# A decoder layer on one core: attention steps in the order scores, filling, values, transposes, filling; the third branch's first inputs in another ring; a variance as float32r

## The chip, the cores and the metric

The kernel runs on one core of a Trainium2 chip. The metric is the device time of one execution in microseconds (us); the lower the better. Each comparison uses several runs, and one further execution is recorded by the hardware profiler. The engines are called as the profile calls them: PE (matrix multiplications), PEld (PE's weight loads), DVE (vector), ACT (scalar), POOL (GpSimd) and SP (the queue that issues most transfers).

## The reference

One layer, 1024 tokens of 1024 channels, float32. It is a feed-forward half step, then a mixer with three branches, then a second feed-forward half step.

```python
u = rms_norm(h, mix_pre_g)
p_rwkv, p_swa, q_mem, gate_logits = _split(u @ w_in, IN_SIZES)
y_a = rwkv7_mix(p_rwkv, ...)                 # recurrence, 8 heads of 64
y_b = sliding_window_gqa_sinks(...)          # window of 128 tokens, 8 heads of 64
y_c = memory_cross_attention(q_mem, ...)     # 256 memory tokens, 4 heads of 128
g_a, g_b, g_c = _split(jax.nn.sigmoid(gate_logits + gate_b), (D, D, D))
merged = g_a * (y_a @ w_branch[0]) + g_b * (y_b @ w_branch[1]) + g_c * (y_c @ w_branch[2])
h = h + rms_norm(merged @ w_out, mix_post_g)
```

`rwkv7_mix` ends with a normalization of each head: the variance over its 64 channels, then a scaling with its reciprocal root.

## The kernel before, in words

Channels lie on the 128 partitions and tokens on the free axis, in halves `h` = 0 and 1 of 512 tokens. A product in full precision is three matrix multiplications in float32r (`mm3`, L348 to L350): weights and inputs are kept as a rounded part `hi` and a rest `lo`, and `hi*hi + hi*lo + lo*hi` is summed in PSUM. ACT makes the `hi` (L277 for weights, L454 for inputs), DVE the `lo` (L279 and L455). A multiplication of plain float32 goes through PE in two passes, and the trace counts both.

The mixer's small, latency-bound pieces (recurrence, normalization, attention) are interleaved by hand with large products. A generator, `filling` (L1252), yields the matmuls of the gates, of the first branch (RWKV, index 0) and of the second (memory, index 2, by `BRANCHES = (0, 2, 1)`). `fill(n, behind)` draws some `n` of them behind a given instruction, in whole steps of its generator. In this part of the program PE's order is the order of the code.

**PSUM.** There are two rings of four banks, `mm` for the large products and `bg` for the rest. Every score bank (`sc`, `msc`), transposed bank (`ptr`, `mptr`) and output bank (`pv`, `mpv`) takes the next of the four `bg` banks and waits until the tile that had it before has been read.

**Attention.** `attention` (L1428) takes 16 blocks of 128 tokens: 8 of memory attention, then 8 of the window. For block `i`, before the change, it calls `values` of block i-1, `turn` of block i, `scores` of block i+1, half of the filling, `load` of block i+2, and the other half. `scores` issues the score matmuls (L93) and the whole softmax: for the window four banks copied by ACT (L126) and DVE (L127), a maximum (L131), the exponentials on ACT, the sum and reciprocal (L138, L139) and eight scalings on DVE (L141). `turn` transposes the probabilities on PE (L96) into two `ptr` banks; ACT copies each (L151), and for window blocks from the second on DVE multiplies each by a mask (L154). `values` multiplies with the values (`pv`) and `y_out` (L1447) copies the result out and sends it to memory `y_d`. `load` brings the queries `qs`, and in a window block the rotation (`rotate`, L1404 to L1406) runs on DVE. One window iteration has 54 matmuls of filling; DVE also works for the filling's weights (L279), for sums of the second feed-forward's weights (`ws`, L611 to L614) and for the first branch's merging (L1492).

**Variance.** `rwkv_finish` (L1190) squares each of 8 halves of the recurrence's output on ACT (L1206, tile `ysq`, three buffers), sums them within each head by a float32 matmul with a matrix of ones (L1213), and takes the logarithm on ACT (L1215), which needs another table of functions first. Filling stands behind each pair: 6, 6 and 12 matmuls, then 30.

**Branches.** `branch_strip` (L1473) loads a gate (`gin`, two buffers), runs 4 `mm3` for each half (`pb`), and multiplies and adds on DVE (L1494) and POOL (L1495). The third branch (the window's) runs in `last_branches` (L1595), first all of h=0 and then all of h=1. `load_y` (L1452) loads its inputs from memory through `x_re` and splits them into 16 tiles `y` of a pool `branch`, which is opened when the pool of the earlier stage, with its `gin` tiles, closes, and takes its place in memory. In the ring `acc` stand the accumulators of the output projection and of the feed-forward parts.

Of the kernel before, what the change touches and what calls it, by code (L numbers as in the profile page):

```python
# [44 lines left out]
BRANCHES = (0, 2, 1)  # L45
# [167 lines left out]
class Builder:  # L213
# [978 lines left out]
    def rwkv_finish(self, pool, y, bonus_d, ya_d):  # L1192

        nc = self.nc
        V, S = nc.vector, nc.scalar
        keep = self.tc.keep_in_program_order
        rs = pool.tile([P, NPAIR, T], F32, name="yrs", bufs=1)
        fin = lambda name: pool.tile([P, TH], F32, tag="fin", name=name, bufs=3)
        halves = [(p, slice(h * TH, (h + 1) * TH)) for p in range(NPAIR) for h in (0, 1)]
        squares = []  # L1200

        def square(i):
            if i < len(halves):
                p, cols = halves[i]
                squares.append(fin("ysq"))
                keep(S.activation(squares[-1], y[:, p, cols], ACT.Square))  # L1206

        square(0)
        square(1)
        self.fill(14, self.behind)  # L1210
        for i, (p, cols) in enumerate(halves):
            ps = self.psum("var")
            end = keep(nc.tensor.matmul(ps, self.bones, squares[i], start=True, stop=True))  # L1213
            square(i + 2)
            keep(S.activation(rs[:, p, cols], ps, ACT.Ln, bias=self.gn_eps, scale=1.0 / C))  # L1215
            if i % 2:
                self.fill(8 if p < NPAIR - 1 else 30, end)
        for p in range(NPAIR):
            keep(S.activation(rs[:, p], rs[:, p], ACT.Exp, scale=-0.5))

        held, self.held = self.held, None
        for f in held:
            f()
        for i, (p, cols) in enumerate(halves):
            bo = fin("bo_in")
            nc.sync.dma_start(bo, bonus_d[p][:, cols])
            r = rs[:, p, cols]
# [24 lines left out]
    def filling(self, u, pool, gate_d, y_d):  # L1252
# [5 lines left out]
            self.unit()  # L1258

        yin = lambda: self.yin.tile([P, TH], F32, tag="yin", name="yin", bufs=4)  # L1260
        load = lambda i: self.load_y(y_d[i], self.u_tile, yin)
        gs = (22, 23)
        ws = [self.strip("win", 24 + g, n > 0) for n, g in enumerate(gs)]
        ps = [{h: self.psum("pgate") for h in (0, 1)} for _ in gs]
        for h in (0, 1):
            for w, p in zip(ws, ps):
                yield from self.project_steps(w, u, {h: p[h]})
            if h == 0:
                y = load(BRANCHES[0])
# [157 lines left out]
    def attention(self, blocks, lumps, others):  # L1427

        blocks[0].load()
        blocks[1].load()  # L1430
        self.fill(50, self.behind)
        self.fill(lumps[0], blocks[0].scores())
        for i, (block, n) in enumerate(zip(blocks, lumps)):
            if i:
                blocks[i - 1].values()
            mm = block.turn()
            if i + 1 < len(blocks):
                mm = blocks[i + 1].scores()
            self.fill(n // 2, mm)
            if i + 2 < len(blocks):  # L1440
                blocks[i + 2].load()
            for f in others.get(i, ()):
                f()
            self.fill(n - n // 2, mm)
        blocks[-1].values()

    def y_out(self, ps, y_d, b, pool):  # L1447
# [1 line left out]
        self.nc.scalar.copy(t, ps.rearrange("p (j c) -> p j c", c=P))  # L1449
        self.nc.sync.dma_start(y_d[:, :, b * P : (b + 1) * P], t)  # L1450

    def load_y(self, y_d, tile, tile_in):  # L1452
        out = [[(tile(), tile()) for _ in range(4)] for _ in (0, 1)]
        for h in (0, 1):
            for k in range(4):
                t = tile_in()
                self.nc.sync.dma_start(t, y_d[:, k, h * TH : (h + 1) * TH])
                self.split(t, *out[h][k])
        return out
# [15 lines left out]
    def branch_strip(self, i, q, w, y, pool, gate_d, mg, halves):  # L1475
# [4 lines left out]
        for o2 in (0, 1):  # L1480
# [8 lines left out]
            for j, h in enumerate(halves):  # L1489
                gh = g[:, j * TH : (j + 1) * TH]  # L1490
                if i == BRANCHES[0]:
                    V.scalar_tensor_tensor(mg[o][h], gh, 1.0, ps[h], ALU.add, ALU.mult)  # L1492
                    continue
                V.scalar_tensor_tensor(gh, gh, 1.0, ps[h], ALU.add, ALU.mult)  # L1494
                nc.gpsimd.tensor_tensor(mg[o][h], mg[o][h], gh, ALU.add)  # L1495

    def mixer_first(self, u, pool, att_d):

# [95 lines left out]
    def last_branches(self, mg, gate_d, y_d):  # L1594

        merged = self.new_u()
        with self.tc.tile_pool(reuse_waits="tile", name="branch", bufs=2) as pool:
            tile = lambda: pool.tile([P, TH], F32R, tag="y", name="y", bufs=16)
            with self.tc.high_priority(offset=self.urgent):
                y = self.load_y(y_d[BRANCHES[2]], tile, self.res_tile)  # L1600
# [179 lines left out]
```

## Time and profile before

| what | value |
|---|---|
| median of 3 runs | 2293.97 us (2291.59 to 2294.14) |
| the profiled execution, its own time | 2295.74 us |
| its span in the trace | 2294.0 us, so 1.7 us lie around it |
| PE busy | 2257.6 us, 98% |
| DVE busy | 1639.5 us, 71% |
| ACT busy | 1001.1 us, 44% |
| POOL busy | 94.2 us, 4% |
| variance matmuls | from 1167.4 to 1179.4 us |
| score matmuls | 1214.1 to 1436.1 us |
| third branch's first half | from 1506.6 us |

Times of the trace are counted from the start of its span. A row of the timeline gives start and duration, engine, line, operation, the tiles written and read, the shape, the number of equal instructions in a row (x), and in brackets how long the engine stood idle before and what released it. PEclk is the share of its full clock that PE was granted.

### The profile page before, as it was taken

Reading aid. Unit: us, or ns where it says so; the run is one execution under the profiler, and the core shown is the slowest. Engines: PE = TensorE matmul, PEld = TensorE weight load, DVE = VectorE, ACT = ScalarE, POOL = GpSimd, SP = SyncE. Lnnn points to the kernel's source line nnn. Section 1 sums busy time; section 2 is a strip of 40 time slices with the busy share of each in tenths; the row PEclk is TensorE's granted clock in tenths of the full one; section 3 lists DMA queues with packets and bytes.
Section 4 is the critical chain, followed back from the end, with each engine's and each line's share of the span. In section 5 each row is a group of like instructions: output and inputs, shape, how many; then the busy total and the mean of one; then the engine's idle time right before and its main releaser. Section 6 shows DMA issues by size and latency. Waiting matters only on the chain. (4 is left out here: it accounts for less than half of the span.)

```text
span 2294.0 us, 33425 instructions
## 1 busy us (share of the span) xinstructions
PE 2257.6 (98%) x11868; PEld 1846.6 (80%) x11868; DVE 1639.5 (71%) x2676; ACT 1001.1 (44%) x1876; POOL 94.2 (4%) x138
## 2 busy tenths in 40 slices
PE   8999999999999999999999999999999999999998
PEld 6788888888788778888878877778788888888887
DVE  6987767666688985994645576675898885656676
ACT  6533333454555653123444454335663233345451
POOL 0000000000000000001300000141000000000000
PEclk9999999999999999999999999999999999999999
DMA  8464666686654466325445678755465552348663
GB/s 285 157 202 165 215 214 213 211 274 199 184 170 148 114 155 189 103 92 182 142 140 175 207 237 277 235 183 160 160 215 180 187 176 92 115 149 256 210 193 119
DMA packets 280774, 417.65 MB, mean 182 GB/s; under 512 B 82304, under 2 KB 104320, under 8 KB 280352
## 3 DMA queue, kind: packets, MB, share of 16 engines
q1 hardware_dynamic: 273408, 400.78, 55.3%
q10 hardware_dynamic: 7200, 14.75, 2.0%
q8 instruction: 93, 1.52, 0.3%
q14 instruction: 73, 0.60, 0.1%
HBM read 284.89 MB, written 129.50 MB: 181 GB/s over the span
## 5 line engine op out<-in xcount | busy, mean ns | idle before, releaser
L277 ACT CAST w_hi<-w_raw 128x512 fp32r<-128x512 f32 x594 | 367.0, 620 | 710.4 <-PE px L349 155.7
L279 DVE TENSOR_TENSOR w_lo<-w_raw,w_hi 128x512 fp32r<-128x512 f32 x594 | 416.3, 703 | 210.8 <-ACT w_hi L277 184.4
L350 PE MATMUL po<-u,w_lo 128*128 128x512 f32 (+1 forms) x476 | 181.5, 381 | 0.0
L348 PE MATMUL po<-u,w_hi 128*128 128x512 f32 (+1 forms) x476 | 181.4, 381 | 0.0
L349 PE MATMUL po<-u,w_hi 128*128 128x512 f32 (+1 forms) x476 | 181.4, 381 | 0.0
L348 PE MATMUL pgate<-u,w_hi 128*128 128x512 f32 x384 | 155.4, 405 | 0.0
L350 PE MATMUL pgate<-u,w_lo 128*128 128x512 f32 x384 | 151.4, 394 | 0.0
L349 PE MATMUL pgate<-u,w_hi 128*128 128x512 f32 x384 | 149.7, 390 | 0.0
L348 PE MATMUL px<-f,w_hi 128*128 128x512 f32 x352 | 137.7, 391 | 2.7 <-DVE up L686 2.6
L348 PE MATMUL px<-u,w_hi 128*128 128x512 f32 x352 | 137.1, 389 | 1.4 <-ACT vm L1377 1.4
L349 PE MATMUL px<-f,w_hi 128*128 128x512 f32 x352 | 137.4, 390 | 0.9 <-DVE f L455 0.9
L348 PE MATMUL pz<-u,w_hi 128*128 128x512 f32 x352 | 137.1, 390 | 0.0
L350 PE MATMUL px<-f,w_lo 128*128 128x512 f32 x352 | 137.1, 389 | 0.0
L349 PE MATMUL pz<-u,w_hi 128*128 128x512 f32 x352 | 137.1, 389 | 0.0
L349 PE MATMUL px<-u,w_hi 128*128 128x512 f32 x352 | 137.0, 389 | 0.0
L350 PE MATMUL px<-u,w_lo 128*128 128x512 f32 x352 | 137.0, 389 | 0.0
L350 PE MATMUL pz<-u,w_lo 128*128 128x512 f32 x352 | 137.0, 389 | 0.0
L455 DVE TENSOR_TENSOR u<-hid,u 128x512 fp32r<-128x512 f32 x114 | 78.2, 690 | 46.1 <-ACT u L454 45.3
L349 PEld LDWEIGHTS po<-u,w_hi 128*128 128x128 f32 x476 | 89.8, 189 | 17.2
L348 PEld LDWEIGHTS po<-u,w_hi 128*128 128x128 f32 x476 | 89.8, 189 | 17.1
L350 PEld LDWEIGHTS po<-u,w_lo 128*128 128x128 f32 x476 | 89.8, 189 | 17.0
L454 ACT CAST u<-hid 128x512 fp32r<-128x512 f32 x114 | 70.6, 620 | 64.1 <-DMA hid<-form_d 56.8
(386 smaller groups left out, 5119.1 us busy)
## 6 DMA issues: line engine op xcount, KB each, us to landing
w_raw<-in_ffn_in SPq DMA_DIRECT2D x220, 256.0 KB
hid<-form_d SPq DMA_DIRECT2D x154, 256.0 KB
w_raw<-in_win SPq DMA_DIRECT2D x112, 256.0 KB
form_d<-g SPq DMA_DIRECT2D x88, 256.0 KB
ws<-in_ffn_out SPq DMA_DIRECT2D x88, 256.0 KB
ffn_sum_d<-ws SPq DMA_DIRECT2D x88, 256.0 KB
w_raw<-ffn_sum_d SPq DMA_DIRECT2D x88, 256.0 KB
form_d<-h SPq DMA_DIRECT2D x66, 256.0 KB
```

What stands on the lines that cost most here:

```text
L277: self.nc.scalar.copy(hi, x)
L279: self.split_last = self.nc.vector.tensor_tensor(lo, x, hi.bitcast(F32), ALU.subtract)
L348: mm(out, wh, xh, start=first, stop=False, **kw)
L349: mm(out, wh, xl, start=False, stop=False, **kw)
L350: mm(out, wl, xh, start=False, stop=last, **kw)
L454: self.nc.scalar.copy(hi, x)
L455: self.nc.vector.tensor_tensor(lo, x, hi.bitcast(F32), ALU.subtract)
```

## The change

Four things change.

1. `rwkv_finish`: the square is made twice, on POOL in float32 (`ysq`) and on ACT rounded to float32r (`ysq_hi`); DVE subtracts to get the rest (`ysq_lo`). Each has two buffers. The sum is two float32r matmuls (with `bones_r`, there already) in place of one float32 matmul. The tag `fin` is left to its other users.
2. `attention`: `scores` of block i+1 and `load` of block i+2 come first, then two thirds (memory) or half (window) of the filling, then `values` of block i-1 and `turn` of block i, then the rest of the filling.
3. `load_y`: the third branch's h=0 tiles come from the ring `acc`; its h=1 tiles stay in the pool `branch`, now with 8 buffers.
4. `branch_strip`: in the second branch the addition of h=0 is on DVE, that of h=1 stays on POOL.

```diff
         def square(i):
             if i < len(halves):
                 p, cols = halves[i]
-                squares.append(fin("ysq"))
-                keep(S.activation(squares[-1], y[:, p, cols], ACT.Square))
+                sq, hi, lo = (pool.tile([P, TH], t, tag=name, name=name, bufs=2) for t, name in ((F32, "ysq"), (F32R, "ysq_hi"), (F32R, "ysq_lo")))
+                nc.gpsimd.tensor_tensor(sq, y[:, p, cols], y[:, p, cols], ALU.mult)
+                keep(S.activation(hi, y[:, p, cols], ACT.Square))
+                V.tensor_tensor(lo, sq, hi.bitcast(F32), ALU.subtract)
+                squares.append((hi, lo))
...
-            end = keep(nc.tensor.matmul(ps, self.bones, squares[i], start=True, stop=True))
+            for n, x in enumerate(squares[i]):
+                end = keep(nc.tensor.matmul(ps, self.bones_r, x, start=n == 0, stop=n == 1))
...
         for i, (block, n) in enumerate(zip(blocks, lumps)):
+            first = n * 2 // 3 if isinstance(block, MemoryBlock) else n // 2
+            if i + 1 < len(blocks):
+                mm = blocks[i + 1].scores()
+                if i + 2 < len(blocks):
+                    blocks[i + 2].load()
+                self.fill(first, mm)
+            else:
+                first = 0
             if i:
                 blocks[i - 1].values()
             mm = block.turn()
-            if i + 1 < len(blocks):
-                mm = blocks[i + 1].scores()
-            self.fill(n // 2, mm)
-            if i + 2 < len(blocks):
-                blocks[i + 2].load()
             for f in others.get(i, ()):
                 f()
-            self.fill(n - n // 2, mm)
+            self.fill(n - first, mm)
...
-    def load_y(self, y_d, tile, tile_in):
-        out = [[(tile(), tile()) for _ in range(4)] for _ in (0, 1)]
+    def load_y(self, y_d, tiles, tile_in):
+        out = [[(tile(), tile()) for _ in range(4)] for tile in tiles]
...
-                nc.gpsimd.tensor_tensor(mg[o][h], mg[o][h], gh, ALU.add)
+                e = V if i == BRANCHES[1] and h == 0 else nc.gpsimd
+                e.tensor_tensor(mg[o][h], mg[o][h], gh, ALU.add)
...
-            tile = lambda: pool.tile([P, TH], F32R, tag="y", name="y", bufs=16)
+            tiles = (lambda: self.qpool.tile([P, TH], F32R, tag="acc", name="y", bufs=16),
+                     lambda: pool.tile([P, TH], F32R, tag="y", name="y", bufs=8))
```

The lines below are the order in which each engine's instructions stand in the two programs; "DMA" rows are transfers that the engine issues, and x counts equal neighbours.

**PE, a window iteration.** Before, values (`pv`), transposes (`ptr`) and the next block's scores (`sc`) stand together between matmuls of filling (`pgate`):

```order
L350 MATMUL pgate<-u,w_lo 128x512
L93 MATMUL pv<-pt,vt 64x256 x4
L96 MATMUL ptr<-ident,sc 128x128 x8
L93 MATMUL sc<-kd_11404,qs 128x256 x4
L93 MATMUL sc<-kd_11405,qs 128x256 x4
L348 MATMUL pgate<-u,w_hi 128x512
```

After, in the first of two places, the scores stand alone:

```order
L350 MATMUL pgate<-u,w_lo 128x512
L93 MATMUL sc<-kd_11444,qs 128x256 x4
L93 MATMUL sc<-kd_11445,qs 128x256 x4
L348 MATMUL pgate<-u,w_hi 128x512
L349 MATMUL pgate<-u,w_hi 128x512
```

and in this block 30 matmuls further on, values and transposes stand together:

```order
L350 MATMUL pgate<-u,w_lo 128x512
L93 MATMUL pv<-pt,vt 64x256 x4
L96 MATMUL ptr<-ident,sc 128x128 x8
L348 MATMUL pgate<-u,w_hi 128x512
L349 MATMUL pgate<-u,w_hi 128x512
```

The scores now come ahead of values and transposes, and filling lies between the transposes and the scores that take their banks.

**DVE, the same stage.** Before, the two mask multiplications of the transposes (L154) stand ahead of the next block's copies of scores (L127):

```order
L139 RECIPROCAL st<-st 128x8
L614 TENSOR_TENSOR ws<-ws 128x512
L141 TENSOR_SCALAR sc<-sc,st 128x128 x8
L279 TENSOR_TENSOR w_lo<-w_raw,w_hi 128x512
L154 TENSOR_TENSOR pt<-ptr,is_own 128x512 x2
L127 COPY_PREDICATED sc<-is_before,sc 128x256 x4
```

After, they still stand directly ahead of such copies, but the block whose probabilities are scaled by the L141 in front of them is the next one, not their own:

```order
L138 TENSOR_TENSOR st<-st 128x8
L139 RECIPROCAL st<-st 128x8
L141 TENSOR_SCALAR sc<-sc,st 128x128 x8
L154 TENSOR_TENSOR pt<-ptr,is_own 128x512 x2
L279 TENSOR_TENSOR w_lo<-w_raw,w_hi 128x512
L127 COPY_PREDICATED sc<-is_before,sc 128x256
```

Thus L154 of a block has moved behind the whole softmax of the block after it.

**ACT, the variance.** Before, the second and third square, the load of the table, the first logarithm, the next square, and a rounding of filling weights:

```order
L1206 ACTIVATE ysq<-y 128x512 x2
L1215 ACT_TABLE_LOAD
L1215 ACTIVATE yrs<-var,gn_eps 128x512
L1206 ACTIVATE ysq<-y 128x512
L277 CAST w_hi<-w_raw 128x512
L1215 ACTIVATE yrs<-var,gn_eps 128x512
```

After:

```order
L1207 ACTIVATE ysq_hi<-y 128x512 x2
L1219 ACT_TABLE_LOAD
L1219 ACTIVATE yrs<-var,gn_eps 128x512
L277 CAST w_hi<-w_raw 128x512
L1207 ACTIVATE ysq_hi<-y 128x512
L1219 ACTIVATE yrs<-var,gn_eps 128x512
```

The table load stands where it stood, behind the third square; with two buffers the third square takes the buffer of the first. The fourth square has moved behind a rounding of weights.

**ACT, the end of the second branch.** Before, the first splits of the third branch's inputs (`y<-x_re`) stand at the end of the row of gate loads and weight roundings:

```order
L277 CAST w_hi<-w_raw 128x512
L1483 DMA gin<-gate_d 128x1024
L277 CAST w_hi<-w_raw 128x512 x2
L454 CAST y<-x_re 128x512
L1483 DMA gin<-gate_d 128x512
L454 CAST y<-x_re 128x512
L1483 DMA gin<-gate_d 128x512
L454 CAST y<-x_re 128x512 x4
```

After, the four of h=0 stand some five gate loads earlier:

```order
L454 CAST y<-x_re 128x512
L277 CAST w_hi<-w_raw 128x512
L454 CAST y<-x_re 128x512
L1490 DMA gin<-gate_d 128x1024
L454 CAST y<-x_re 128x512
L277 CAST w_hi<-w_raw 128x512
L454 CAST y<-x_re 128x512
L1490 DMA gin<-gate_d 128x1024
```

The four have moved from behind the second branch's last gate load into the middle of that branch.

More of the change, by code (lines that the diff above doesn't have):

```diff
@@ L1260, in filling @@
         yin = lambda: self.yin.tile([P, TH], F32, tag="yin", name="yin", bufs=4)
-        load = lambda i: self.load_y(y_d[i], self.u_tile, yin)
+        load = lambda i: self.load_y(y_d[i], (self.u_tile, self.u_tile), yin)
         gs = (22, 23)
@@ L1597, in last_branches @@
         with self.tc.tile_pool(reuse_waits="tile", name="branch", bufs=2) as pool:
-            tile = lambda: pool.tile([P, TH], F32R, tag="y", name="y", bufs=16)
+            tiles = (lambda: self.qpool.tile([P, TH], F32R, tag="acc", name="y", bufs=16),
+                     lambda: pool.tile([P, TH], F32R, tag="y", name="y", bufs=8))
             with self.tc.high_priority(offset=self.urgent):
-                y = self.load_y(y_d[BRANCHES[2]], tile, self.res_tile)
+                y = self.load_y(y_d[BRANCHES[2]], tiles, self.res_tile)
             for h in (0, 1):
```

## The prediction

> **What bounds the kernel now.** I first read the page: PE is busy nearly all the time, and it also leads the chain that ended last. Then its pitch in an undisturbed stretch of 200 us, from the table by window (columns: busy time and matmuls of PE, PEld, DVE, ACT, POOL, then PEclk, DMA share, GB/s):
>
> ```profile
> span 2294.0 us, 33425 instructions
> PE 2257.6 (98%) x11868; PEld 1846.6 (80%) x11868; DVE 1639.5 (71%) x2676; ACT 1001.1 (44%) x1876; POOL 94.2 (4%) x138
> 200.00:400.00 200.00, 200.00 (x884) 165.64 (x884) 144.36 (x232) 74.58 (x127) 0.00 (x0) 1.00 0.62 203
> ```
>
> So 200/884 = 0.226 us per 512-column matmul is the price of a slot on PE, and a change helps only where PE does fewer passes, stands idle, or runs at a lower clock. The list of PE's waits names four in the stages that the change touches:
>
> ```profile
> PE sc L93 <- DVE pt L154: 1.7, 1, 1.7
> PE pb L349 <- DVE y L455: 1.5, 1, 1.5
> PE pb L348 <- ACT y L454: 1.0, 1, 1.0
> PE pb L348 <- DVE gin L1494: 0.5, 1, 0.5
> PE mptr L96 <- DVE mp L192: 0.4, 1, 0.4
> ```
>
> (The fifth, 0.4 before the memory transposes, is the first block's.) "Busy" also hides lost time: where two interleaved row groups of PE can't both run, or the clock is low, the bar stays full. For that I read the table by window, PE alone, over the 16 score matmuls of consecutive blocks, and over two stretches of low clock:
>
> ```profile
> 1321.12:1323.15 2.03, 2.03 (x17) 1.00 1.06 320
> 1337.67:1340.41 2.74, 2.74 (x17) 1.00 0.95 308
> 1355.83:1358.58 2.75, 2.75 (x17) 1.00 0.93 316
> 1374.00:1376.68 2.68, 2.68 (x17) 1.00 0.92 292
> 1392.10:1396.17 4.07, 3.91 (x17) 1.00 0.96 334
> 1411.59:1416.63 5.04, 3.35 (x17) 1.00 0.91 257
> 1433.66:1436.41 2.75, 2.75 (x17) 1.00 1.07 334
> 1417.00:1420.50 3.50, 3.50 (x10) 0.53 0.86 279
> 1509.40:1512.80 3.40, 3.40 (x8) 0.50 0.78 237
> ```
>
> The first scores follow transposes of a memory block, whose banks only ACT reads, and take 2.03 us. The other six follow window transposes, and their third and fourth bank must wait until DVE has multiplied the mask (L154). The worst of them, in order of time:
>
> ```profile
> 1412.91 0.69 DVE L612 TENSOR_TENSOR ws<-ws 128x512 f32<-128x512 f32 x1
> ...
> 1413.64 0.69 DVE L613 TENSOR_TENSOR ws<-ws 128x512 f32<-128x512 f32 x1
> 1414.25 1.28 DVE L154 TENSOR_TENSOR pt<-ptr,is_own 128x512 f32<-128x512 f32 x2
> ...
> 1414.99 1.72 PE L93 MATMUL sc<-kd,qs 64*128 64x256 f32 x8 [1.69 <-DVE pt L154]
> ```
>
> DVE had sums for the feed-forward ahead of L154, PE stood for 1.69 us, and 2 us later the clock fell to 0.53 for 3.5 us.
>
> **Attention order.** The six disturbed score groups take 2.74 + 2.75 + 2.68 + 4.07 + 5.04 + 2.75 = 20.03 us; at 2.03 each they would take 12.18. That is 7.85. The low clock costs (1 - 0.53) x 3.5 = 1.65, and the 0.4 before `mptr` goes, as filling now lies ahead of those transposes. Sum 9.9. No matmul is added, and the transitions between shapes only move.
>
> What is late next is DVE. In the new order L154 of block i stands behind the softmax of block i+1, whose last part is the eight scalings L141. The longest softmax before, from PE's first score to the last L141:
>
> ```profile
> 1392.11 4.14 PE L93 MATMUL sc<-kd,qs 64*128 64x256 f32 x16
> 1405.07 0.69 DVE L1404 TENSOR_TENSOR qs<-qs,cos 128x512 f32<-128x512 f32 x1 [5.14 <-DMA qs<-att_d]
> 1409.26 0.68 DVE L141 TENSOR_SCALAR sc<-sc,st 128x128 f32<-128x128 f32 x3
> 1335.50:1352.80 17.30, 17.30 (x87) 13.31 (x86) 12.34 (x30) 8.64 (x28) 0.00 (x0) 1.00 0.70 237
> ```
>
> From 1392.11 to 1409.94 is 17.8 us, 5.14 of it a wait for queries that a transfer brings while the transfers are saturated. L154 adds 1.28, so 19.1. The next block's scores start an iteration later, 17.3 by the shortest iteration in the last row, and want their third bank after about half of 2.03: at 18.3. This block would lose 0.8; a second one, whose softmax I estimate from the same rows at 1 us shorter, nothing or up to 0.5. I take 1.3 for both. Bounds: nothing, if the softmax shrinks with its scores (4.07 to 2.03) and the queries, now loaded ahead of the first half of the filling on SP's queue, land earlier; 7, if every block loses 1. Net gain **8.6**, between 3 and 9.9.
>
> **Variance.** PE's time per pair of halves:
>
> ```profile
> 1167.38 1.88 PE L1213 MATMUL var<-ysq,bones 128*128 128x512 f32 x4
> 1168.69 0.79 PE L348 MATMUL pgate<-u,w_hi 128*128 128x512 f32 x1
> 1169.33 0.40 PE L349 MATMUL pgate<-u,w_hi 128*128 128x512 f32 x1
> ```
>
> From the first pass to the second filling matmul are 1.95 us for five slots; at 0.226 they take 1.13. Four pairs gain 4 x 0.82 = 3.3. Against it stands a new chain, POOL square, ACT square, DVE rest. ACT's rows of before give its pace:
>
> ```profile
> 1164.86 1.28 ACT L1215 ACT_TABLE_LOAD   x1
> 1168.44 0.69 ACT L1215 ACTIVATE yrs<-var,gn_eps 128x512 f32<-128x512 f32 x1 [2.29 <-PE var L1213]
> 1169.02 0.62 ACT L1206 ACTIVATE ysq<-y 128x512 f32<-128x512 f32 x1
> 1170.45 0.62 ACT L277 CAST w_hi<-w_raw 128x512 fp32r<-128x512 f32 x1 [0.81 <-PE pgate L349]
> ```
>
> The table load lay in idle time before the first `var`. With two buffers the third square must wait until PE has read the first (about 1167.9), and the load stands behind it: square to 1168.5, load to 1169.8, logarithm (0.6) to 1170.4, rounding to 1170.9, fourth square to 1171.5, its rest (0.69 on DVE) to 1172.2. PE wants that fourth half after 4 matmuls, 6 of filling and 2 more, at 1167.4 + 12 x 0.226 = 1170.1: a stall of 2.1. Later halves are paced by POOL and DVE:
>
> ```profile
> 1477.96 1.28 POOL L1495 TENSOR_TENSOR u<-u,gin 128x512 f32<-128x512 f32 x1 [0.94 <-DVE gin L1494]
> 1478.07 1.73 DVE L279 TENSOR_TENSOR w_lo<-w_raw,w_hi 128x512 fp32r<-128x512 f32 x1 [0.19 <-ACT w_hi L277]
> ```
>
> A POOL operation of this shape takes 1.28, and a DVE subtraction beside it 1.73 in place of 0.69. I take 0.9 more stall, and 0.2 for the first rest, which DVE gets inside the recurrence behind POOL. So -3.3 + 2.1 + 0.9 + 0.2 = **about 0**. Bounds: -3.3 with no stall, and +2.5 if the 2.1 is followed by a low clock as the 1.69 above was, with a price of 1.65 and more contention.
>
> [...]
>
> **Third branch.** Its first matmuls before:
>
> ```profile
> 1505.43 0.62 ACT L277 CAST w_hi<-w_raw 128x512 fp32r<-128x512 f32 x1 [4.82 <-PE pb L349]
> ...
> 1505.95 1.66 ACT L454 CAST y<-x_re 128x512 fp32r<-128x512 f32 x3
> ...
> 1506.62 1.20 PE L348 MATMUL pb<-y,w_hi 128*128 128x512 f32 x4 [1.05 <-ACT y L454]
> 1507.51 4.76 DVE L455 TENSOR_TENSOR y<-x_re,y 128x512 fp32r<-128x512 f32 x6
> ...
> 1508.74 1.66 ACT L454 CAST y<-x_re 128x512 fp32r<-128x512 f32 x3 [1.13 <-POOL u L1495]
> ...
> 1509.31 0.79 PE L349 MATMUL pb<-y,w_hi 128*128 128x512 f32 x1 [1.50 <-DVE y L455]
> ```
>
> PE stood for 1.05 and 1.50, then had half its clock for 3.4 us (1.70 lost): 4.25 together. The splits waited for the place of the `gin` tiles, which POOL's last addition gave free. In the ring `acc` they wait for no `gin`, and the order has them in the middle of the second branch. The h=1 tiles are in the old place, but are wanted 96 matmuls later, 21.7 us, which covers the same lateness; were that cover gone, 4.25 would come back. The four splits move ahead of weight roundings on ACT and DVE, which adds some 0.6 of ACT to each; the first row shows ACT idle for 4.82 ahead of such a rounding, so nothing is charged. Gain **4.25**, between 3 and 5.
>
> **Additions on DVE.** Eight of 0.69 in place of eight of 1.28 on POOL; they free the `gin` buffer earlier, so some of the 0.5 wait for L1494 goes. I take 0.3, between 0 and 0.6.
>
> [...]
>
> **Sum.** 8.6 + 0 + 4.25 + 0.3 = 13.2 off the profiled execution's 2295.74 us gives 2282.5. That execution is 1.8 above the median of the runs shown, in which frame it is 2280.8. I predict 2281.
>
> **Rivals.**
> - *All of it, variance included.* No stall in the variance and none behind the softmax: 9.9 + 3.3 + 4.25 + 0.6 = 18 off, 2276. For it: DVE is busy for 12.3 of 17.3 us per iteration. Against: the table load has no other place in the order.
> - *Attention's gain is given back.* L154 behind the softmax is late by 1 us in each of seven iterations: 7 lost, 2287. For it: 19.1 against 18.3 in one block. Against: the worst one holds the 5.14 of a transfer.
> - *Slower.* The same chain, in every window iteration more than 1.7 us late, the point from which the clock fell before: that is 20.0 from first score to the end of L154, 0.9 above the longest. Seven times 1.7 + 1.65 is 23.5, against gains of 14.45, so 9 slower: 2303. For it: softmax, rotation, `ws` sums and roundings share one queue in order, and faster scores make transfers collide earlier. Against: the longest is already the one with the late transfer.
> - *Nothing happens.* The waits move to the transfers that feed them (the shares of 0.9 to 1.07 in the scores' windows), and time stays near 2294.
>
> **How the numbers follow.** Forecast 0.60; all of it 0.13; given back 0.13; slower 0.08; nothing 0.06. A measurement of this kernel can tell about 0.2% (4.6 us) from no change. Faster than that are the first two and most of the third, 0.84; within it the fourth and the rest, 0.08; slower 0.08. The range goes from 2274 (every gain at its upper bound: 9.9 + 3.3 + 5 + 0.6 = 18.8, and about 1.5 of spread) to 2290 (attention 3, third branch 3, variance +2, which is 4 off the median), leaving out the slower case, no effect, and little else.
>
> **What would show it.** Score groups of 2.0 to 2.1 us in all window blocks, no wait `sc <- DVE pt` above 1 us, PEclk at 1.00 around 1410 and 1505; the first `pb<-y` without idle time; in the variance a wait of about 2 us at the fourth half for DVE's `ysq_lo`, with the table load just ahead of it. I am wrong if `sc` waits for L154 in most iterations, or if the variance shows a low clock, or if POOL's squares hold DVE for longer than 2 us.

## The result, and the profile after

| kernel | median, us | runs | ratio to the kernel before, 95% interval |
|---|---|---|---|
| before | 2294.18 | 12 | |
| changed | 2290.53 (2287.52 to 2296.09) | 12 | 0.9985 (0.9976 to 0.9993) |
| changed, once more (with runs of before of its own, 2294.56) | 2288.42 (2286.57 to 2292.07) | 8 | 0.9973 (0.9963 to 0.9984) |

By the ratios the change makes the kernel faster by 3.4 us in the first comparison and by 6 in the second; neither interval reaches 1. The sign was forecast, the size was not: the prediction said 2281 and its range ended at 2290. The page of the changed kernel:

```profile
span 2292.4 us, 33449 instructions
PE 2251.3 (98%) x11868; PEld 1844.1 (80%) x11868; DVE 1650.7 (72%) x2692; ACT 998.8 (44%) x1876; POOL 92.1 (4%) x138
```

PE's waits in the changed stages (us in total, times, longest):

```profile
PE pb L348 <- DVE gin L1501: 2.9, 4, 2.0
PE sc L93 <- DVE pt L154: 1.8, 1, 1.8
PE var L1217 <- ACT ysq_hi L1207: 1.2, 1, 1.2
PE var L1217 <- DVE ysq_lo L1208: 0.3, 1, 0.3
```

Both waits of the third branch's first inputs (1.5 and 1.0) are gone. The wait of the scores for L154 is still there, the one for the second branch's multiplications has grown from 0.5 to 2.9, and the variance has two new ones. The table by window, PE alone, shows the score groups of four window blocks, and three stretches of low clock (the other three score groups take 2.03 us too):

```profile
1337.33:1339.36 2.03, 2.03 (x17) 1.00 0.82 257
1388.84:1390.87 2.03, 2.03 (x17) 1.00 0.80 289
1406.87:1411.60 4.73, 2.90 (x17) 0.99 0.54 185
1428.60:1430.63 2.03, 2.03 (x17) 1.00 0.99 302
1176.10:1179.50 3.40, 3.40 (x10) 0.52 0.08 31
1411.60:1415.00 3.40, 3.40 (x9) 0.51 0.68 226
1483.20:1486.60 3.40, 3.35 (x8) 0.50 0.86 277
```

So the order does what it was forecast to do in every score group but one, and each of the three longest of these waits (1.2 + 0.3, 1.8 and 2.0 us) is followed by half clock.

To see where the time went I took the start of the same matmul in both traces at the edges of each stage, and the difference of the stage's length (after minus before, us). PE does the same work between those edges, apart from the variance's passes.

| stage | before | changed | again | forecast |
|---|---|---|---|---|
| variance: end of the recurrence to `gup` | 23.62 | +0.42 | +0.38 | 0 |
| attention: first `msc` to the second branch's first product | 244.50 | -5.81 | -5.59 | -8.6 |
| second branch, from the last `pv` to its end | 39.23 | +3.42 | +5.38 | -0.3 |
| third branch's start: end of the second to a quarter of the third | 16.08 | -4.75 | -4.75 | -4.25 |
| third branch's second half, to the output projection | 21.76 | +1.06 | +0.31 | 0 |
| sum | | -5.66 | -4.27 | -13.2 |

Stages that the change doesn't touch moved as well, by some 2 us each and in both signs (424 us of the first feed-forward half step by +2.17 and -0.24 in the two executions), which I take for the scatter of single executions. I therefore read stages by their traces and whole kernels by their medians.

### The profile page after: what moved, and what is told of

It is laid out like the page before. It is cut to its first block, busy times and chain, and to the rows that moved or that the text cites. A ratio compares the mean times of both kernels' runs of the same rounds, so it can differ in the third digit from the quotient of the medians.

```text
span 2292.4 us, 33449 instructions
## 1 busy us (share of the span) xinstructions
PE 2251.3 (98%) x11868; PEld 1844.1 (80%) x11868; DVE 1650.7 (72%) x2692; ACT 998.8 (44%) x1876; POOL 92.1 (4%) x138
## 4 chain that ended last, share of the span: by engine, by line
PE 75%; DVE 13%; DMA 6%; issue 2%; ACT 2%; POOL 0%; SPq 0%; ACTq 0%; DVEq 0%; POOLq 0%
PE po L349 6%; PE po L348 6%; PE po L350 6%; PE px L348 5%; PE px L349 5%; PE px L350 5%; PE pgate L348 3%; PE pgate L350 3%; PE pgate L349 3%; DMA w_raw<-in_ffn_in 3%; PE pz L349 2%; PE pz L348 2%; PE pz L350 2%; DVE w_lo L279 2%; PE pq L350 1%
## 5 line engine op out<-in xcount | busy, mean ns | idle before, releaser
L279 DVE TENSOR_TENSOR w_lo<-w_raw,w_hi 128x512 fp32r<-128x512 f32 x594 | 411.5, 694 | 201.9 <-ACT w_hi L277 184.3
L455 DVE TENSOR_TENSOR u<-hid,u 128x512 fp32r<-128x512 f32 x114 | 78.2, 690 | 46.7 <-ACT u L454 44.6
L350 PEld LDWEIGHTS po<-u,w_lo 128*128 128x128 f32 x476 | 89.5, 188 | 17.1
```

The source lines that it names most:

```text
L279: self.split_last = self.nc.vector.tensor_tensor(lo, x, hi.bitcast(F32), ALU.subtract)
L350: mm(out, wl, xh, start=False, stop=last, **kw)
L455: self.nc.vector.tensor_tensor(lo, x, hi.bitcast(F32), ALU.subtract)
```

## The experiments

The theory after the first traces: the variance, the attention and the third branch's start do what was forecast, except that one block's softmax became longer; and the early splits of the third branch hold up the second branch. The rivals: the new additions on DVE make the second branch wait; or the gates (`gin`), of which the kernel holds two at a time, arrive late; or all this is chance of an execution.

### Each part alone

e1 to e4 are the kernel before with one part of the change: the order of attention, the variance, the ring, and the additions.

```diff
 e1_order: part 2 alone
+            if i + 1 < len(blocks):
+                mm = blocks[i + 1].scores()
 e2_var: part 1 alone
+                nc.gpsimd.tensor_tensor(sq, y[:, p, cols], y[:, p, cols], ALU.mult)
+                V.tensor_tensor(lo, sq, hi.bitcast(F32), ALU.subtract)
 e3_ring: part 3 alone
+            tiles = (lambda: self.qpool.tile([P, TH], F32R, tag="acc", name="y", bufs=16),
 e4_add: part 4 alone
+                e = V if i == BRANCHES[1] and h == 0 else nc.gpsimd
```

> The kernel before with the new attention order alone. Theory T (the profile of the change read stage by stage): the order takes 20.0 us of window scores to 6 x 2.03 but in one block L154 stands behind a softmax that waits about 4 us for a gate of the first branch, and PE stands 1.8 us and then runs at half clock; the stage gains about 5.8 us, so 2288.4 against 2294.2. Rival R1: that one stall comes from the other edits (shifted transfers), and alone the order gains 8.6 to 9.5, about 2285. Rival R2: the order gains less than 3.

> The kernel before with the variance in float32r alone. Theory T: four pairs gain 3.3 us, the fourth half waits 1.2 to 1.5 us behind the table load and the clock halves after it (1.7 us), so the stage ends within 0.5 us of before and the time is 2294 +- 1. Rival R1: the wait and the low clock were chance of that execution; then about 2291. Rival R2: slower by over 2.

> The kernel before with the third branch's h=0 tiles in the accumulators' ring alone; all additions of the second branch stay on POOL. Theory T (early splits are the cost): the third branch starts 4.75 us earlier, but the splits of y now stand on DVE ahead of the second branch's multiplications L1494, and PE waits some 2 us there, with half clock after it: 3.4 us back, net -1.3, about 2293. Rival R1 (the additions on DVE are the cost): the wait in the second branch stays at 0.5 as before, net -4.75, 2289.4.

> The kernel before with the second branch's h=0 additions on DVE alone. Theory T: within 0.5 us of before, PE's wait for L1494 0.5 or less. Rival R1 (the additions on DVE are the cost of the new wait): PE waits about 2 us for the multiplications in the second branch and the time is 2 to 3.5 us longer.

Measured, with the stages' differences to before:

| kernel | median, us | ratio (interval) | variance | attention | second branch | third's start | its second half |
|---|---|---|---|---|---|---|---|
| e1_order | 2289.97 | 0.9984 (0.9972 to 0.9996) | 0.0 | -5.91 | +0.66 | +1.18 | 0.0 |
| e2_var | 2294.49 | 1.0007 (0.9995 to 1.0020) | -1.15 | -1.22 | -0.27 | +1.25 | +0.83 |
| e3_ring | 2295.94 | 1.0009 (0.9997 to 1.0021) | 0.0 | +1.54 | +2.59 | -4.75 | +3.54 |
| e4_add | 2294.62 | 1.0005 (0.9995 to 1.0015) | 0.0 | -2.71 | +1.32 | -1.64 | +0.91 |

The order alone is worth all that the whole change is worth, and it has its one slow score group (4.70 us) without the other parts, as T said. The variance alone changes nothing that can be told; its stage is 1.15 shorter, since the wait came as in T and the low clock behind it did not. The ring gains exactly 4.75 at the place it was made for, and gives back 2.59 and 3.54 in the two stages beside it; T's waits in the second branch came (1.66 and 1.27 us), their half clock did not, and the time is 3 us above T's 2293. The additions alone are within noise, though their trace has a wait of 2.15 us in the second branch: the wait that R1 named, without the price that R1 gave it. No low clock followed it. Stages that a part does not touch move by up to 2.7 (attention in e4), so single differences below that are not evidence.

### Additions back on POOL

```diff
-                e = V if i == BRANCHES[1] and h == 0 else nc.gpsimd
-                e.tensor_tensor(mg[o][h], mg[o][h], gh, ALU.add)
+                nc.gpsimd.tensor_tensor(mg[o][h], mg[o][h], gh, ALU.add)
```

> The changed kernel with all of the second branch's additions back on POOL. Theory T (the wait in the second branch has two parents: the gate loads, which have two buffers and land late, and the splits of y and the additions that stand between two multiplications on DVE): PE's waits for L1494's counterpart stay above 1 us in sum, the time within 2 us of the changed kernel's 2290.5. Rival R1 (the additions alone are the cost): the 2.0 us wait near 1483 and the low clock after it go, 3.4 us faster, 2287.

2287.22 us, 0.9977 (0.9964 to 0.9989), within noise of the changed kernel. The second branch is 4.74 us longer than before (waits of 1.41 and 2.51), as with the additions. The additions on DVE are not the cost of that branch's waits. Its third branch's second half is 3.71 us longer than before, as in e3 (3.54), where these additions are on POOL too; in the five traces with the ring, two gates and the additions on DVE it is 0.00 to 1.06 longer. That would be worth more than the 0.3 of the prediction, but the median of e5 is not above that of the changed kernel, so what the additions are worth stays open.

### Scalings behind the transposes

```diff
             mm = block.turn()
+            if i + 1 < len(blocks) and isinstance(blocks[i + 1], WindowBlock):
+                blocks[i + 1].scale()   # L138 to L141, taken out of scores()
```

> The changed kernel, but the sum, reciprocal and eight scalings of the next window block (L138 to L141) are issued after the transposes, so that on DVE the mask multiplication L154 stands ahead of them. Theory T (L154 is late because it stands behind a softmax that waits for a gate): the 1.8 us wait near 1409 and the low clock go, all six score groups take 2.03 us, the attention stage gains another 2.7 to 3.5 us, 2287.5. Rival R1 (the DVE queue ahead of L154 is late anyway, since the wait for the gate stands ahead of both): the wait stays within 0.5 us of 1.8. Rival R2: the scalings come late for the next transposes and a wait moves there.

2279.71 us, 0.9946 (0.9934 to 0.9957), attention -9.66 and a slowest group of 2.99. The stage gains another 3.85 us where T had 2.7 to 3.5, and yet not by T's mechanism; the median lies 7.8 below T's 2287.5, which attention alone does not explain. DVE's rows of this run (its lines stand 4 to 6 below those of the changed kernel, so L1505 is the first branch's merging, L1412 and L1414 the rotation, L146 the scaling and L158 the mask):

```profile
1395.86 0.69 DVE L1505 SCALAR_TENSOR_TENSOR u<-gin,pb 128x512 f32<-128x512 f32 x1 [5.27 <-DMA gin<-gate_d]
1396.91 0.69 DVE L1412 TENSOR_TENSOR qs<-qs,cos 128x512 f32<-128x512 f32 x1 [0.37 <-DMA qs<-att_d]
...
1398.68 1.46 DVE L146 TENSOR_SCALAR sc<-sc,st 128x128 f32<-128x128 f32 x7
1400.06 1.28 DVE L158 TENSOR_TENSOR pt<-ptr,is_own 128x512 f32<-128x512 f32 x2
```

Seven of eight scalings still stand ahead of the mask: in the order as built they are back where they were. What differs is when the gate and the queries came. In the changed kernel the slow block's rows on DVE and PE are these (L1499 merging, L1408 and L1410 rotation, L141 scaling):

```profile
1405.24 0.69 DVE L1499 SCALAR_TENSOR_TENSOR u<-gin,pb 128x512 f32<-128x512 f32 x1 [4.12 <-DMA gin<-gate_d]
...
1405.85 0.69 DVE L1408 TENSOR_TENSOR qs<-qs,cos 128x512 f32<-128x512 f32 x1
...
1406.57 0.69 DVE L1410 TENSOR_TENSOR qs<-qs,qsw 128x512 f32<-128x512 f32 x1
...
1407.61 1.66 DVE L141 TENSOR_SCALAR sc<-sc,st 128x128 f32<-128x128 f32 x8
1409.18 1.28 DVE L154 TENSOR_TENSOR pt<-ptr,is_own 128x512 f32<-128x512 f32 x2
...
1409.92 1.29 PE L93 MATMUL sc<-kd,qs 64*128 64x256 f32 x6 [1.83 <-DVE pt L154]
```

DVE stands 4.12 us for a gate; behind it, in order, are the rotation of the queries, the softmax's sums, its scalings and the mask that PE waits for. This block's scores began at 1388.84, so its scalings ended 20.4 us later, and in e6 19.5 (its scores began at 1381.99). The merging behind the gate starts 16.4 us after the first score here and 13.9 in e6, the rotation 17.0 and 14.9. My T was wrong about what to move; the run says only that the stall shrinks when the two transfers come earlier after the scores.

### Gates in half tiles

```diff
-            g = pool.tile([P, T], F32, tag="gate", name="gin", bufs=2)[:, :n]
-            nc.scalar.dma_start(g, gate_d[i * KD + o][:, cols])
+            g = {h: pool.tile([P, TH], F32, tag="gate", name="gin", bufs=4) for h in halves}
+            for h in halves:
+                nc.scalar.dma_start(g[h], gate_d[i * KD + o][:, h * TH : (h + 1) * TH])
```

> The changed kernel with the gates (gate, gin and the attention inputs of the same ring) in four tiles of half the width in place of two, each loaded and freed by itself, so that where a step needs only half a gate two more loads can be under way. Theory T (two buffers make the gate loads late, and late gates hold DVE): the waits for gates on DVE near 1400 and 1480 and PE's waits for the multiplications of the second and third branch shrink; second branch -3, third branch's second half -1, attention -2 to -3.5; 2284. Rival R1 (the transfers are late because they are saturated, not because they are issued late): nothing gained, 2290 +- 1.5.

2286.65 us, 0.9975 (0.9966 to 0.9985). The second branch is 1.12 us shorter than before in place of 3.42 longer: late gates do hold it, as T says. Attention (-5.72, slowest group 5.51) didn't move and the third branch's second half is 1.84 longer: there T failed. DVE's rows in the slow block (L1501 merging, L1408 rotation) say why attention stayed:

```profile
1397.47 0.69 DVE L1501 SCALAR_TENSOR_TENSOR u<-gin,pb 128x512 f32<-128x512 f32 x1 [0.49 <-DMA gin<-gate_d]
1402.95 0.69 DVE L1408 TENSOR_TENSOR qs<-qs,cos 128x512 f32<-128x512 f32 x1 [4.79 <-DMA qs<-att_d]
```

The gate now comes 11.6 us after the first score, but DVE then stands 4.79 us for the queries, and the rotation starts at 17.1, as late as in the changed kernel. Late queries alone are enough for the slow group.

### The table earlier

```diff
         square(1)
+        keep(S.activation(rs[:, 0, :1], self.gn_eps, ACT.Ln))
         self.fill(14, self.behind)
```

> The changed kernel with one more logarithm of one column ahead of the filling, so that ACT loads its table before the third square and not behind it. Theory T: the fourth half's wait falls from 1.5 to about 0.5 us and the clock stays up; the variance stage is 2.5 us shorter than with the float32 variance and 2.9 shorter than in the changed kernel; 2287.6. Rival R1 (the wait comes from POOL and DVE): it stays above 1 us.

2286.06 us, 0.9970 (0.9959 to 0.9982); the variance stage is 2.20 us shorter than before, as T forecast within 0.3, and its one wait is

```profile
PE var L1218 <- DVE ysq_lo L1208: 0.4, 1, 0.4
```

### All three, with and without the ring

e9 joins the edits of e6, e7 and e8. e10 is e6 with the third branch's tiles in their old pool. e11 is e9 with eight half gates in the third branch, in the memory that the ring frees. e12 is e9 with the old pool.

```diff
 e11_deep:
+            tag, bufs = ("gin", 8) if i == BRANCHES[2] else ("gate", 4)
 e10_noring, e12_allnoring:
-            tiles = (lambda: self.qpool.tile([P, TH], F32R, tag="acc", name="y", bufs=16),
+            tile = lambda: pool.tile([P, TH], F32R, tag="y", name="y", bufs=16)
```

> The changed kernel with three mends together: scalings after the transposes, gates in four half tiles, the table loaded ahead of the filling. Theory T (three separate causes, which add): attention -9.7, variance -2.2, second branch about -1, third branch's start -4.75, its second half +1 to +2, sum -15 to -16.5 against the stages of before; 2277 against 2293. Rival: a gate or a transfer takes up what a mend frees, and it stays within 1.5 us of the 2279.7 of the scalings alone.

> The changed kernel with the scalings after the transposes, and with the third branch's h=0 tiles back in the pool of before. Theory T (with two gate buffers the early splits give back in the second branch what the ring gains): the third branch's start loses 4.75 us again, the second branch's wait of 2 us and its low clock go (-3.9), the rest alike: within 2 us of the 2279.7 with the ring. Rival R1 (the second branch's wait has nothing to do with the ring): 4 to 5 us slower, 2284.

> All three mends, and eight half tiles for the third branch's gates in the memory that the h=0 tiles left. Theory T (late gates make the waits in the third branch's second half): its stage returns to before, 1 to 2 us faster than with four; 2275.5. Rival: DVE's own queue makes these waits, and nothing changes.

> All three mends, and the third branch's h=0 tiles back in the pool of before. Theory T (with four half gates the ring gives back nothing): 4.5 to 5 us slower than with the ring and all three mends, about 2281.5. Rival: within 1.5 us of it, the ring is worth nothing either way.

| kernel | median, us | ratio (interval) | attention | second branch | third's start | its second half | sum of the last three |
|---|---|---|---|---|---|---|---|
| e6: ring, two gates | 2279.71 | 0.9946 (0.9934 to 0.9957) | -9.66 | +4.52 | -4.75 | +0.73 | +0.50 |
| e10: no ring, two gates | 2284.29 | 0.9969 (0.9959 to 0.9980) | -3.04 | -1.12 | -1.66 | +0.10 | -2.68 |
| e9: ring, four half gates | 2284.45 | 0.9966 (0.9952 to 0.9979) | -4.18 | -1.12 | -4.75 | +2.27 | -3.60 |
| e12: no ring, four half gates | 2287.27 | 0.9982 (0.9971 to 0.9992) | -3.81 | -1.12 | -1.67 | +2.04 | -0.75 |
| e11: ring, eight in the third branch | 2281.42 | 0.9952 (0.9939 to 0.9965) | -5.38 | -1.12 | -4.75 | +0.49 | -5.38 |

By medians all four missed what T gave (2277, within 2 us of 2279.7, 2275.5 and about 2281.5), because the slow score group is back in all of them (6.43, 6.21, 5.95 and 7.77 us): they hold e6's edit, so e6's gain does not come with its edit. The stages beside attention answer the question about the ring in part. In the pair e6 and e10, with two gates, the ring costs 3.2 us in its three stages (+0.50 against -2.68), but that is within the scatter: over all traces with two gates the three stages add up to between -2.96 and +3.70 with the ring (seven traces) and to between -2.68 and +1.85 without it (five, before among them). One stage is clear of the scatter: the second branch is 1.45 to 5.38 longer in the seven, and between -1.12 and +1.32 in the five. With four half gates it is 1.12 shorter with the ring and without, and the ring gains 2.9 in the three stages (-3.60 against -0.75), while e9's and e12's medians differ by 2.8 where T had 4.5 to 5. e11 shows what ends its second half: deeper gates take 1.8 us off.

### The two transfers

```diff
 e13_spin, e14_both, e15_best: rotation held behind the mask L154
+        keep(V.tensor_tensor(x, x, cos, ALU.mult))       # rotate, called after turn()
+                keep(self.nc.vector.tensor_tensor(self.pt[:, 1, i : i + 4], ps, own, ALU.mult))
 e14_both, e15_best: query load earlier on SP (both have half gates)
-        nc.sync.dma_start(self.qs, src)
+        with self.k.tc.high_priority(offset=60): nc.sync.dma_start(self.qs, src)
```

e15 has the early table and the eight half gates as well; e16 is the changed kernel again.

> The changed kernel with the rotation of the queries on DVE held behind the mask multiplication L154 of the block before. Theory T (either of two late transfers alone holds the softmax, gate or query): the gate still stands ahead of the sums, and the one slow score group stays above 4 us; 2290 +- 2. Rival R1 (the queries alone): the score groups all take 2.03 to 2.1, attention -9, 2287. Rival R2: the next block's queries are rotated late and a wait moves to the scores themselves.

> The changed kernel with half-width gates, the query load issued ahead of the stores of the feed-forward sums, and the rotation held behind L154. Theory T: neither transfer stands ahead of L154, all window score groups take 2.03 to 2.1 us, attention -9 to -9.7 against before, and with the second branch's gain the time is 2282. Rival: a group above 4 us stays, and the cause is a third one (the exponentials, or the weights).

> e14_both with the table loaded early and eight half gates in the third branch. Theory T: attention -9 to -9.7, variance -2.2, second branch -1.1, third branch -4.75 and +0.5: -16.5 to -17 against the stages of before, 2276. Rival: 2281, as without the two edits on the queries.

> The changed kernel once more. Theory T: the same waits at the same places, the slow score group within 1 us of 4.7, second branch +3 to +4, and 2290.5 +- 1. Rival: the waits come and go between executions, and a stage moves by over 2 us.

| kernel | median, us | ratio (interval) | variance | attention | second branch | third's start | its second half |
|---|---|---|---|---|---|---|---|
| e13_spin | 2281.46 | 0.9942 (0.9930 to 0.9953) | -1.18 | -8.49 | +1.45 | -4.75 | +0.33 |
| e14_both | 2281.76 | 0.9940 (0.9928 to 0.9952) | -1.17 | -9.50 | -1.12 | -4.75 | +2.80 |
| e15_best | 2277.96 | 0.9928 (0.9914 to 0.9942) | -2.24 | -9.53 | -1.12 | -4.75 | 0.00 |
| e16_again | 2288.42 | 0.9973 (0.9963 to 0.9984) | +0.38 | -5.59 | +5.38 | -4.75 | +0.31 |

With the rotation held back no score group is slow (2.03 six times, 2.00 in the slow block). So for e13 T's forecast failed and R1's came (attention -8.49 for -9, the time 5.5 below its 2287); R2's came too, the wait moves to the rotated queries. The run does not show the rotation alone, though, for its gate came early as well. DVE's rows (L1500 merging, L141 scaling, L154 mask, L1408 rotation; the first score is at 1382.27):

```profile
1396.03 0.69 DVE L1500 SCALAR_TENSOR_TENSOR u<-gin,pb 128x512 f32<-128x512 f32 x1 [5.07 <-DMA gin<-gate_d]
...
1397.07 1.66 DVE L141 TENSOR_SCALAR sc<-sc,st 128x128 f32<-128x128 f32 x8
1398.64 1.28 DVE L154 TENSOR_TENSOR pt<-ptr,is_own 128x512 f32<-128x512 f32 x2
1399.84 0.68 DVE L1408 TENSOR_TENSOR qs<-qs,cos 128x512 f32<-128x512 f32 x1
```

The merging starts 13.8 us after the first score, not 16.4 as in the changed kernel. Of the 3.9 us by which the scalings end earlier, 2.6 are the gate's and 1.3 the rotation's. e6, with its gate at 13.9, is the closer pair for the rotation: there the mask ends 19.4 us after the first score, here 17.7, and the slowest group falls from 2.99 to 2.03. What a gate as late as 16.4 would do without the rotation was not run. e14 and e15 came within 0.3 and 2 us of T's 2282 and 2276, without a slow group. PE's waits of e13:

```profile
PE sc L93 <- DVE qs L1410: 2.1, 1, 2.1
PE pb L348 <- DVE gin L1502: 2.0, 1, 2.0
```

and of e15, which is the fastest kernel of the study by its median and its ratio (its interval overlaps that of e6):

```profile
PE sc L93 <- DVE qs L1411: 1.0, 1, 1.0
PE var L1218 <- DVE ysq_lo L1208: 0.4, 1, 0.4
```

In the slow block, from the first score to the end of the scalings, the traces show 17.8 us before, 20.4 to 23.4 in ten executions of the new order, 19.5 in e6, and 16.5, 15.5 and 15.4 in e13, e14 and e15. e16 repeats the changed kernel's long waits at the same places, so the stall is no chance. Its sizes are less sure than T had them: the second branch is 5.38 longer (T: 3 to 4) and the median 2.1 lower.

## Why the prediction was wrong, point by point

**Attention, right in kind, 2.8 us short.** Six groups, 7.85 to gain: all but one now take 2.03, and the 0.4 before `mptr` is gone. The step that failed is the one that took the longest softmax over from before: "L154 adds 1.28, so 19.1", against a want at 18.3, and a loss of 0.8, 1.3 for both blocks. The one slow group lost 2.7 us (4.73 for 2.03) and the low clock behind it 1.7. The 19.1 was measured from a start that the change moves. The scores now begin a half filling earlier in the stream, while the transfers do not come as much earlier. SP's rows around the query load, before:

```profile
1394.57 3.91 SPq L616 DMA_DIRECT2D ffn_sum_d<-ws  x4
1398.53 0.61 SPq L603 DMA_DIRECT2D ws<-in_ffn_out  x1
1399.23 0.55 SPq L105 DMA_DIRECT2D qs<-att_d  x1
```

and after:

```profile
1396.30 3.12 SPq L616 DMA_DIRECT2D ffn_sum_d<-ws  x4
1399.47 0.57 SPq L603 DMA_DIRECT2D ws<-in_ffn_out  x1
1400.21 0.55 SPq L105 DMA_DIRECT2D qs<-att_d  x1
```

The same four stores of DVE's sums, for which SP's queue stood 1.0 us before and 0.4 after around this block, and the same load stand ahead of it. From the first score (1392.11 before, 1388.84 after) the load is issued after 7.1 us before and after 11.4 now, and the rotation starts after 13.0 and 17.0. "The queries, now loaded ahead of the first half of the filling on SP's queue" is how the code reads; in the order that was recorded the load is not ahead. In this trace the gate ahead of the rotation is the last to come (16.4, against at most 13.6 before); in e7, e9, e11 and e12, where it comes after 9.8 to 12.0, the rotation stands for the queries until 17.1 to 18.6. The softmax then ends at 20.4, the mask 1.2 later at 21.6, PE stands for 1.83 us, and the low clock that followed, which I had priced only for the waits that go, takes back what the one that went had cost. Why the transfers come when they do is not shown beyond SP's rows.

**Second branch, wrong by 3.7 us, and by 5.7 in the second execution.** The step is "nothing is charged" for the splits that move into it. The changed kernel's rows of DVE and PE at the longest wait (L1501 multiplication, which frees a bank; L455 split of `y`; L279 weights; L1503 addition):

```profile
1479.50 0.69 DVE L1501 SCALAR_TENSOR_TENSOR gin<-gin,pb 128x512 f32<-128x512 f32 x1 [2.64 <-DMA gin<-gate_d]
1480.11 0.68 DVE L455 TENSOR_TENSOR y<-x_re,y 128x512 fp32r<-128x512 f32 x1
...
1480.71 0.69 DVE L279 TENSOR_TENSOR w_lo<-w_raw,w_hi 128x512 fp32r<-128x512 f32 x1
1481.31 0.69 DVE L455 TENSOR_TENSOR y<-x_re,y 128x512 fp32r<-128x512 f32 x1
1481.91 0.69 DVE L1503 TENSOR_TENSOR u<-u,gin 128x512 f32<-128x512 f32 x1
1482.51 1.88 DVE L1501 SCALAR_TENSOR_TENSOR gin<-gin,pb 128x512 f32<-128x512 f32 x3
...
1483.25 0.80 PE L348 MATMUL pb<-u,w_hi 128*128 128x512 f32 x1 [2.04 <-DVE gin L1501]
```

A late gate, then four operations of 0.69 between two multiplications, and PE without a free bank for 2.04 us and at half clock after it. ACT's idle 4.82, on which I had rested, says nothing of DVE's moments behind a late gate. e10 (no ring) and e7 (more gates) each take the loss away; e5 (no additions) doesn't. So it takes the ring and the two gate buffers together; the seven traces that have both are 1.45 to 5.38 longer, the least of them (e13) with the same wait of 2.04 and no low clock. Whether the splits' time on DVE or the loads of `x_re` that go with them weigh more was not separated.

**Third branch, right at its start** (-4.75 for -4.25). The 1.70 of low clock in that sum is not always there to be gained: in e4, e10 and e12, without the ring, it did not come, and the start is 1.64 to 1.67 shorter than before, with the same waits. Its second half, priced at nothing because its tiles have 21.7 us of cover, had the tiles in time; what waited there was again a multiplication for a gate (+1.06 and +0.31; 0.00 in e15, whose gates are deep).

**Variance, right in size** (+0.42 for 0), in part by luck. ACT and PE of the changed kernel:

```profile
1170.40 0.63 ACT L1207 ACTIVATE ysq_hi<-y 128x512 fp32r<-128x512 f32 x1 [3.49 <-PE var L1217]
1171.05 1.28 ACT L1219 ACT_TABLE_LOAD   x1
1172.34 0.69 ACT L1219 ACTIVATE yrs<-var,gn_eps 128x512 f32<-128x512 f32 x1
1172.93 0.61 ACT L277 CAST w_hi<-w_raw 128x512 fp32r<-128x512 f32 x1
1173.43 0.63 ACT L1207 ACTIVATE ysq_hi<-y 128x512 fp32r<-128x512 f32 x1
```

```profile
1174.12 0.49 PE L1217 MATMUL var<-ysq_hi,bones_r 128*128 128x512 f32 x1 [1.23 <-ACT ysq_hi L1207]
1174.91 0.50 PE L1217 MATMUL var<-ysq_lo,bones_r 128*128 128x512 f32 x1 [0.30 <-DVE ysq_lo L1208]
```

The third square waits for a buffer, the table load stands behind it, and the fourth square comes late: that chain is as forecast. But PE waits 1.53 us where I had 2.1, there is none of the later 0.9, and what makes up for them is a low clock of some 1.6 us, which my sum left out and which I had named as a sign of being wrong. It came in the two executions of the changed kernel and in e5 and e10 (+0.4 each) and not in e2, e6, e7, e13 and e14 (about -1.2 each). Two errors of one size cancel. e8, where the table is loaded early and the wait falls to 0.4, confirms the table load as the cause of the wait. One rest on DVE took 1.51 us beside a square on POOL, where the median rest took 0.69. That didn't set the stage's length, as PE waited 0.30 us in all for rests.

**The rivals.** "Attention's gain is given back" had the right mechanism, in one block and not in seven. The second branch as the place of a loss was in none of them, and the upper end of the range lacked it. The forecast that the kernel gets faster was right; the 13.2 of the sum came to 5.7 and 4.3 in the stages of the two executions.

## What to carry to other kernels

When a step is moved ahead, measure the chain behind it from its new start: a transfer that does not move with it comes later after it (here the load was issued after 11.4 us in place of 7.1), and code that issues a load sooner did not place it sooner here, in a queue ordered by a scheduler. A transfer's late arrival (4.12 us of DVE's time for one gate) was paid by everything behind it on DVE, so look for unrelated operations (here a merging and a rotation) between a chain's links. Before inputs are prepared earlier, look at the shallow ring beside them: with two gate buffers it made the second branch 1.5 to 5.4 us longer, with four half buffers the branch took no harm and the ring gained 2.9 in all.

## What the runs showed of the hardware that I had not expected

The low clock is not a price that each long wait pays. It followed waits of 1.69 us before and of 1.83, 2.04 and 1.23 + 0.30 us in the changed kernel; it did not follow 2.15 us in e4, nor 2.06 and 2.04 in e13, whose table by window after these two waits reads

```profile
1401.90:1405.30 3.40, 3.40 (x22) 1.00 0.75 224
1473.60:1477.00 3.40, 3.40 (x15) 1.00 0.84 275
```

The slow stretches lie on a grid. In the record of the granted clock that the trace holds, PE has 0.50 for 3.41 us from 621.89, 1417.19 and 1509.35 us before, and from 844.88, 1175.97, 1411.49 and 1483.17 us in the changed kernel; one more, of over 9 us, runs to the end of each program. Divided by 3.413 us, the recorded length of each of these stretches, the distances between these starts are 233.0 and 27.0 before and 97.0, 69.0 and 21.0 after: whole numbers in both traces. Below, a window is 3.41 us on this grid.

Which of the long waits were followed by half clock went with where they fell on it. Before, the windows with 1.21 and 2.18 us of idle time of PE were followed by half clock, those with 1.48 and 0.74 were not; in the changed kernel those with 1.83, 1.53, 1.83 and 2.32 were, the one with 1.00 was not. PE's idle time in each window, counted from 800 to 1600 us in all 18 traces where the clock was full, sorts them: all 12 windows with over 1.9 us idle were followed by half clock, 15 of the 47 with 1.2 to 1.9, and none of the 44 with 0.6 to 1.2. The second branch's wait of 2.04 us lies in one window in e8, whose clock halved, and is split into 1.55 and 0.49 in e13, whose clock stayed. The third branch's two waits put 2.18 us into one window before, and 1.05 and 1.43 into two in e4, where no low clock came. What decides between 1.2 and 1.9 us stays open, and no run shifted a wait to try it. For a forecast I estimate from these counts a chance of some 1.7 us (half of 3.41) for each wait of 1.2 us or more, not a certainty.
